# New homes for the merged stream's transposes, for two tail units of the output projection and for the convolved projections' weights

## The chip, the cores and the metric

One Trainium2 chip; the kernel runs on one of its cores. The metric is the device time of one execution in microseconds. The core's engines are named as the profile names them: PE (matmuls; PEld is its weight load), DVE (vector), ACT (scalar activations and copies), POOL, and SP, which issues most DMAs.

## The reference

Two layers of a decoder trunk, 256 tokens, model width 1024, all in float32. Cut to what matters:

```python
def hybrid_layer(x, mem_n, ...):
    h = layer_norm(ALPHA * x + 0.5 * swiglu(x, ffn1_w_gu, ffn1_w_down), ...)
    dn_q, dn_k, dn_v, dn_b, dn_a, dn_z, sw_q, sw_k, sw_v, xa_q, gates = split(h @ w_in)
    o_dn = deltanet_branch(dn_q, dn_k, dn_v, ...)   # q, k, v: silu(causal 4-tap convolution over time)
    o_sw = sliding_window_attention(sw_q, sw_k, sw_v, swa_sinks)
    o_xa = memory_cross_attention(xa_q, mem_n, w_mem_kv)
    merged = sum over the 3 branches of sigmoid(gates) * (branch @ w_branch)
    h = layer_norm(ALPHA * h + merged @ w_out, ...)
    return layer_norm(ALPHA * h + 0.5 * swiglu(h, ffn2_w_gu, ffn2_w_down), ...)
```

The normalised q and k of the DeltaNet branch need sums of squares over each head's 128 channels, for which the kernel transposes them to tokens.

## The kernel before

All weights lie in one long stream in memory, in the order of their use, and are read as units of 128 partitions × 1024 floats (512 KB). `unit()` (line 104) takes the next one: SP loads it into one of four `raw` buffers, and `split` (line 121) writes a high part by a cast on ACT (`whi`) and the rest by a subtract on DVE (`wlo`). A product of two split operands is three matmuls on PE: high·high, high·low, low·high (`mm3`). Without `dst` the two parts go to rings of five buffers each, `whi` and `wlo`; with `dst` they go to named tiles, their homes. The cast of a unit can begin when the load has landed and the last reader of its home is through; the load when a `raw` buffer is free, that is after an earlier unit's subtract.

Where a tile lies in a partition (an address inside the 192 KB of each) is settled by its pool: `hT` (the transposed, split activations, moving or stationary operand of the projections) and `u0` to `u9` lie in a low pool, below 74 KB, then come `whi` and `wlo` (74 to 115 KB), and `w0` to `w3`, `u10` to `u13` lie in a high pool, from 149 KB on.

In `mixers` (line 514) PE's instructions are pinned to program order; the other compute engines get an order from a scheduler that goes by priority, and `unit()` asks for its instructions 300 places ahead. Each engine then runs its own list in order. SP's loads keep program order.

The stages that matter here:

- The conv stage (lines 535 to 590): `conv` for k, q, v, in this order. Each is two halves of two units; a unit is 24 matmuls of 256 columns (stationary the weights, moving `hT`; the profile's names for a matmul's inputs give the moving operand first). Each half goes through `use`: a scale on ACT (L540), three taps on DVE (L543) for each of its two blocks, and a silu on ACT (L544) into the transposed kT, qT or vT (`u0`, `u1`, `u8`). In between stand the transposes to tokens on PE: `tok_k` behind the third unit of q, `tok_q` behind the third unit of v (L133, 8 transposes each), followed by squares on ACT (L564) and reductions on DVE (L565). The next projections of `hT` (xq and sw's q and k) follow.
- The merge (lines 975 to 1037): `branch(2, oT)` multiplies the last branch's output by its weights; for each of four banks DVE applies the gate (L988) and POOL adds it to the merged stream `mg` (L990); `merge_turn` transposes `mg` on PE (L133) into `sm` banks, two of which there are, and splits it into four tiles `mgT`, two for the high and two for the low part.
- The output projection (line 1040): `projA` over 8 units; two lead ones go through `whi`/`wlo`, and six tail units have homes of their own. Stationary operand is `mgT`, moving the weights, 512 columns a matmul. `between(0)` makes the last `merge_turn` and ends the pinning.

Places in the conv stage are told by numbers that the program gives its tiles: conv units 8 to 11 (v) have the raw buffers 2396, 2426, 2467 and 2514, the five units behind them 2600, 2630, 2663, 2705 and 2738; `t_417` and `t_430` are q's halves, `t_438` and `t_450` v's.

Of the kernel before, what the change touches and what calls it, by code (L numbers as in the profile page):

```python
# [2 lines left out]

# [1 line left out]

# [6 lines left out]
F32R = mybir.dt.float32r  # L12
# [5 lines left out]
P = 128  # L18
D = 1024
S = 256  # L20
# [18 lines left out]
def tile_trunk(ctx, tc, x, xT, mem, memT_, wst, lnp, memln, cvw, rows, cst, out):  # L39
# [6 lines left out]
    pu = ctx.enter_context(tc.tile_pool(name="pu", bufs=1))  # L46
# [8 lines left out]
    def nm(s):  # L55
        uid[0] += 1
        return f"{s}_{uid[0]}"
# [4 lines left out]
    def T(pool, shape, tag, dt=F32, bufs=None):  # L62
        pool = pn if pool is pu and tag in NEAR else pool
        kw = {} if bufs is None else {"bufs": bufs}
        return pool.tile(shape, dt, tag=tag, name=nm(tag), **kw)

    def acc():
        return T(psA, [P, 512], "acc")
# [35 lines left out]
    def unit(w=U, dst=None, cuts=1, behind=None):  # L104
        ahead = tc.high_priority(offset=AHEAD) if pos[0] >= 8 * P * U else nullcontext()
        raw = T(praw, [P, U], "raw")
        src = wst[pos[0]:pos[0] + P * w].rearrange("(p w) -> p w", p=P)
        pos[0] += P * w
        (ph, th), (pl, tl) = dst or ((phi, "whi"), (plo, "wlo"))
        with ahead:  # L110
            hi = T(ph, [P, U], th, F32R)
            lo = T(pl, [P, U], tl, F32R)
            for i in range(cuts):
                c = slice(i * w // cuts, (i + 1) * w // cuts)
                nc.sync.dma_start(raw[:, c], src[:, c])
                with tc.issue_after(behind) if behind else nullcontext():
                    newest[:] = split(hi[:, c], lo[:, c], raw[:, c])
        return hi, lo

    def split(hi, lo, src):  # L120
        return nc.scalar.copy(hi, src).ins, nc.vector.tensor_tensor(lo, src, hi.bitcast(F32), op=ALU.subtract).ins  # L121
# [7 lines left out]
    def matmul(*a, **k):  # L129
        return pe(nc.tensor.matmul(*a, **k))  # L130
# [16 lines left out]
    def projB(xt, nt, kpu, behind=None):  # L147
        g = projB_parts(xt, nt, kpu, behind)
        while True:
            try:  # L150
                next(g)
            except StopIteration as e:
                return e.value

    def projB_parts(xt, nt, kpu, behind=None):
        banks = [acc().rearrange("p (t s) -> p t s", t=2) for _ in range((nt + 1) // 2)]
        for uu in range(KD // kpu):
            hi, lo = unit(behind=behind)
            for kk in range(kpu):
                k = uu * kpu + kk  # L160
                for t in range(nt):
                    c = (kk * nt + t) * P
                    o = banks[t // 2][:, t % 2, :]
                    lastt = t % 2 == 1 or t == nt - 1
                    matmul(o, hi[:, c:c + P], xt[0](k), start=(k == 0 and t % 2 == 0), stop=False, skip_group_check=True)
                    matmul(o, hi[:, c:c + P], xt[1](k), start=False, stop=False, skip_group_check=True)
                    matmul(o, lo[:, c:c + P], xt[0](k), start=False, stop=(k == KD - 1 and lastt), skip_group_check=True)
            yield
        return banks

    def halves(xt, use):

        for i in range(2):
            (b,) = yield from projB_parts(xt, 2, 4)
            use(i, b)

    def projA(xt, w, kpu, nk, outs, tail=0, dsts=(), lead=0, after=None, behind=None, held=(), led=None, along=None, ends=()):
# [46 lines left out]
    def full_rows():  # L224

        a, b, c, d = (acc() for _ in range(4))
        return [[a, b], [c, d]], [at()[:, 0:S] for _ in range(2)]
# [13 lines left out]
    def acc_of(t):  # L241
        return (lambda k: t[0][:, k, :], lambda k: t[1][:, k, :])

    def to_T(put, tb, src, q):

        ps = sm()
        for j in range(4):
            k = q * 4 + j
            transpose(ps[:, j * P:(j + 1) * P], src[:, k * P:(k + 1) * P], ident)
        hi, lo = put(q)  # L250
        ts = slice(tb * P, (tb + 1) * P)
        split(hi[:, :, ts], lo[:, :, ts], ps.rearrange("p (j t) -> p j t", j=4))
# [261 lines left out]
    def mixers(l, hT, mkT, mv_, post):  # L514
        xt = acc_of(hT)
# [7 lines left out]
        for tb in range(2):  # L523
            a, b = outs[tb]
# [7 lines left out]

        silu = []

        def conv(seg, dst):
            def use(i, b):
                yc = T(p2, [P, 2, S], "t2", bufs=4)
                for j in range(2):
                    w = cw[:, l, seg * 4 + 2 * i + j, :]
                    nc.scalar.activation(yc[:, j, :], b[:, j, :], AF.Copy, scale=w[:, 3:4])  # L540
                    for t in (2, 1, 0):
                        d = 3 - t
                        nc.vector.scalar_tensor_tensor(yc[:, j, d:], b[:, j, :S - d], w[:, t:t + 1], yc[:, j, d:], op0=ALU.mult, op1=ALU.add)  # L543
                silu[:] = [nc.scalar.activation(dst[:, 2 * i:2 * i + 2, :], yc, AF.Silu).ins]  # L544
            return halves(xt, use)


        kT, qT, vT = (T(pu, [P, 4, S], tag) for tag in ("u0", "u1", "u8"))
# [34 lines left out]
        def tok_q():  # L583
            for tb in range(2):
                sumsq(tok(qT, tb), ssq[:, 1, tb, :])
            nc.vector.tensor_scalar(qeps, ssq[:, 1], RMS_EPS, RMS_EPS * P, ALU.add, ALU.mult)

        weave(conv(1, kT), {})
        weave(conv(0, qT), {3: [tok_k]})
        weave(conv(2, vT), {3: [tok_q]})  # L590


# [218 lines left out]
        def use_sq(i, b):  # L811
            split(*(t[:, 2 * i:2 * i + 2, :] for t in sq_), b)

        weave(halves(xt, use_xq), {3: [tok_v]})
        (b,) = projB(xt, 1, 8)
        for kv in range(2):
            hs = slice(kv * 64, kv * 64 + 64)
            split(swk[0][hs, kv, :], swk[1][hs, kv, :], b[hs, 0, :])
        weave(halves(xt, use_sq), {
            1: [decay],  # L820
            2: [lambda: spread(0), lambda: x_scores(0)],
# [133 lines left out]
        mg, mgT, gts = [], [], {}  # L955
# [68 lines left out]

        def merge_turn(tb, q):
            if not mgT:
                mgT.extend(T(pu, [P, 4, S], f"w{i}", F32R) for i in range(4))
            to_T(lambda q: (mgT[q], mgT[2 + q]), tb, mg[tb], q)

        weave(branch(2, oT), {  # L1030
            3: [lambda: merge_turn(0, 0)],
            4: [lambda: merge_turn(0, 1), lambda: merge_turn(1, 0)]})

        def between(tb):
            if tb == 0:
                merge_turn(1, 1)
                pinned[0] = False

        outs, ends = full_rows()
        projA((lambda k: mgT[k // 4][:, k % 4, :], lambda k: mgT[2 + k // 4][:, k % 4, :]), D, 1, KD, outs, 6,  # L1040
              [((pu, a), (pu, b)) for a, b in (("u6", "u7"), ("u10", "u11"), ("u12", "u13"), ("u0", "u1"), ("u2", "u3"), ("u8", "u9"))], 2, post, led=between, ends=ends)


    hT = new_hT()
# [25 lines left out]
    ends = None  # L1070
    for l in range(NL):
        mT = []
        mid = memory_T(mT, l)
        if l == 0:

            more = {4: lambda *a: xres(0), 6: lambda *a: xres(1), 8: lambda *a: small()}
        post = Post(lnp[l, 0, 0], lnp[l, 0, 1])
        f1.rest(hT, 4, [((pu, "u0"), (pu, "u1")), ((pu, "u2"), (pu, "u3"))], post, mid, ends, {} if l else more)
        kv = memory_kv(mT, post.end)
        if l == 0:  # L1080
            nc.scalar.activation(nea, rw[:, :, 8:12], AF.Exp)
            nc.vector.tensor_scalar(nea, nea, -1.0, None, ALU.mult)
        post2 = Post(lnp[l, 1, 0], lnp[l, 1, 1])
        mixers(l, post.hT, *kv, post2)
        f2 = Ffn()
        begin(f2, post2.hT)
        last = l == NL - 1
        post = Post(lnp[l, 2, 0], lnp[l, 2, 1], last)
        f2.rest(post2.hT, 6, [((pu, a), (pu, b)) for a, b in (("u0", "u1"), ("u2", "u3"), ("u4", "u5"), ("u6", "u13"))], post, behind=post2.end)
        ends = post.end  # L1090
        if not last:
            f1, hT = Ffn(), post.hT
            begin(f1, hT)
# [87 lines left out]
```

## Time and profile before

| | us |
|---|---|
| median of 3 runs | 1281.85 (1281.18 to 1282.19) |
| the profiled execution | 1281.28 |
| its span in the profile | 1279.5 |
| PE busy in it | 1262.5 (99%) |
| DVE busy | 865.1 (68%) |
| ACT busy | 660.3 (52%) |
| POOL busy | 210.9 (16%) |
| mean granted PE clock | 0.997 |

The span begins and ends with the first and last instruction; the execution's own time is 1.8 us longer. All places in time below are us from the span's start. In the rows of a timeline the columns are start, length, engine, line, operation, output<-inputs, shapes, the number of instructions, and in brackets the idle time of the engine just before and what ended it.

### The profile page before, as it was taken

The page shows a single profiled execution, that of the slowest core. Times are in us where ns is not written, and L with a number is a line of the kernel's source. Part 1 is how long each engine was busy: PE and PEld are TensorE (multiplying, and loading weights), DVE is VectorE, ACT ScalarE, POOL GpSimd, SP SyncE. Part 2 cuts the span into 40 slices and gives each one's busy share as a digit, 9 for nine tenths or more (in the row PEclk, how much of TensorE's full clock was granted, in tenths as well). Part 3 has the DMA queues.
Part 4 walks back from the last instruction along what each step waited for, and adds up shares of the span by engine and source line. Part 5 has one row for each costly group of instructions (what it writes and reads, how often), then busy time and mean ns, then how long its engine had stood idle before and what let it go on. Part 6 is the DMA issues. An engine that isn't in the chain of part 4 may idle for free.

```text
span 1279.5 us, 18763 instructions
## 1 busy us (share of the span) xinstructions
PE 1262.5 (99%) x6948; PEld 1074.8 (84%) x6948; DVE 865.1 (68%) x1271; ACT 660.3 (52%) x980; POOL 210.9 (16%) x365
## 2 busy tenths in 40 slices
PE   9999999999999999999999999999999999999997
PEld 6888889999878788888888888899987787888886
DVE  6678576886647776665676665759867388766565
ACT  6556444655665535444454554456656654445441
POOL 0232000002311202221012220010033102122200
PEclk9999999999999999999999999999999999999999
DMA  8888765655434728886657876456464266487762
GB/s 297 304 272 283 254 206 163 210 166 139 160 116 151 260 90 266 243 240 217 227 200 246 256 253 220 176 186 210 152 164 137 95 194 218 168 242 245 236 224 86
DMA packets 77499, 261.40 MB, mean 204 GB/s; under 512 B 11904, under 2 KB 13056, under 8 KB 77408
## 3 DMA queue, kind: packets, MB, share of 16 engines
q1 hardware_dynamic: 66320, 232.53, 55.4%
q0 software_dynamic: 11088, 27.68, 8.1%
q8 instruction: 54, 0.88, 0.3%
q14 instruction: 37, 0.30, 0.1%
HBM read 246.40 MB, written 13.76 MB: 203 GB/s over the span
## 4 chain that ended last, share of the span: by engine, by line
PE 93%; DVE 2%; DMA 2%; ACT 1%; issue 1%; POOL 0%; SPq 0%; DVEq 0%; ACTq 0%; POOLq 0%
PE acc L130 82%; PE at L130 4%; PE sm L130 3%; DMA raw<-in_wst_dram 2%; PE sm L133 1%; DVE wlo L121 1%; PE acc L323 1%; PE acc L324 1%; PE acc L326 1%; ACT whi L121 1%; PE at L133 1%; DVE u L121 0%; POOL u L990 0%; ACT u L121 0%; DVE gt L988 0%
## 5 line engine op out<-in xcount | busy, mean ns | idle before, releaser
L121 DVE TENSOR_TENSOR wlo<-raw,whi 128x1024 fp32r<-128x1024 f32 (+2 forms) x403 | 488.3, 1220 | 281.0 <-ACT whi L121 279.2
L121 ACT CAST whi<-raw 128x1024 fp32r<-128x1024 f32 (+2 forms) x403 | 412.7, 1033 | 399.2 <-PE acc L130 318.8
L130 PE MATMUL acc<-whi,hT 128*128 128x512 f32 (+1 forms) x1824 | 562.6, 386 | 0.6 <-ACT whi L121 0.6
L130 PEld LDWEIGHTS acc<-whi,hT 128*128 128x128 f32 x1824 | 340.2, 188 | 70.0 <-ACT whi L121 2.4
L130 PE MATMUL acc<-wlo,hT 128*128 128x512 f32 (+1 forms) x912 | 350.2, 384 | 0.7 <-DVE wlo L121 0.7
L130 PE MATMUL acc<-whi,u 128*128 128x512 f32 x784 | 248.9, 392 | 0.0
L130 PEld LDWEIGHTS acc<-wlo,hT 128*128 128x128 f32 x912 | 171.3, 188 | 33.9 <-DVE wlo L121 1.7
L130 PEld LDWEIGHTS acc<-whi,u 128*128 128x128 f32 x784 | 147.2, 188 | 30.6
L130 PE MATMUL acc<-wlo,u 128*128 128x512 f32 x392 | 152.7, 390 | 0.0
L353 POOL DMA_DIRECT2D tr<-t x176 | 96.5, 555 | 303.7 <-DVE t L347 293.2
L130 PE MATMUL acc<-hT,whi 128*128 128x256 f32 x672 | 122.2, 284 | 0.0
L130 PEld LDWEIGHTS acc<-hT,whi 128*128 128x128 f32 x672 | 104.6, 192 | 0.0
L130 PE MATMUL acc<-hT,wlo 128*128 128x256 f32 x336 | 95.0, 283 | 0.0
L130 PEld LDWEIGHTS acc<-wlo,u 128*128 128x128 f32 x392 | 73.7, 188 | 14.8
L130 PEld LDWEIGHTS acc<-hT,wlo 128*128 128x128 f32 x336 | 64.3, 191 | 0.0
L354 POOL DMA_DIRECT2D pt<-tr x44 | 25.1, 570 | 199.1 <-DMA tr<-t 133.1
L344 ACT ACTIVATE t<-acc 128x256 f32<-128x256 f32 x88 | 33.5, 381 | 37.7 <-PE acc L130 37.6
L990 POOL TENSOR_TENSOR u<-u,gt 128x512 f32<-128x512 f32 x16 | 24.3, 1527 | 131.1 <-DVE gt L988 131.1
L345 DVE TENSOR_TENSOR t<-t,acc 128x256 f32<-128x256 f32 x88 | 36.6, 416 | 8.8 <-ACT t L344 5.3
L121 DVE TENSOR_TENSOR u<-pt,u 128x512 fp32r<-128x512 f32 x44 | 28.9, 657 | 15.9 <-ACT u L121 15.9
L121 ACT CAST u<-pt 128x512 fp32r<-128x512 f32 x44 | 27.0, 613 | 18.3 <-DMA pt<-tr 18.3
L121 DVE TENSOR_TENSOR u<-raw,u 128x1024 fp32r<-128x1024 f32 x24 | 30.9, 1290 | 7.9 <-ACT u L121 7.8
(236 smaller groups left out, 1210.1 us busy)
## 6 DMA issues: line engine op xcount, KB each, us to landing
raw<-in_wst_dram SPq DMA_DIRECT2D x409, 512.0 KB, 4.4
tr<-t POOLq DMA_DIRECT2D x176, 64.0 KB, 3.9
pt<-tr POOLq DMA_DIRECT2D x44, 256.0 KB, 5.1
raw<-in_wst_dram SPq DMA_DIRECT2D x16, 324.0 KB, 2.9
gB<-in_lnp_dram SPq DMA_DIRECT2D x6, 512.0 KB, 5.6
bB<-in_lnp_dram SPq DMA_DIRECT2D x6, 512.0 KB, 6.0
w<-dr POOLq DMA_DIRECT2D x4, 512.0 KB, 10.7
t<-in_xT_dram SPq DMA_DIRECT2D x4, 256.0 KB, 5.2
```

The costliest lines, as they stand in the source:

```text
L121: return nc.scalar.copy(hi, src).ins, nc.vector.tensor_tensor(lo, src, hi.bitcast(F32), op=ALU.subtract).ins
L130: return pe(nc.tensor.matmul(*a, **k))
L133: return pe(nc.tensor.transpose(*a))
L323: nc.tensor.matmul(ps, hT[0][:, k, ts], hi[:, c], start=k == 0, stop=False)
L324: nc.tensor.matmul(ps, hT[0][:, k, ts], lo[:, c], start=False, stop=False)
L326: nc.tensor.matmul(ps, hT[1][:, k, ts], hi[:, c], start=False, stop=k == KD - 1)
L344: act = nc.scalar.activation(t[:, :, tb, :], g, AF.Silu).ins
L345: ins = nc.vector.tensor_tensor(t[:, :, tb, :], t[:, :, tb, :], u, op=ALU.mult).ins
L353: nc.gpsimd.dma_start(d[:, :, q].rearrange("b c x -> c b x"), z[32 * q:32 * q + 32].rearrange("c (b x) -> c b x", b=4))
L354: back = nc.gpsimd.dma_start(y, d.rearrange("b c q x -> (b c) (q x)")).ins
L990: nc.gpsimd.tensor_tensor(mg[tb][:, js], mg[tb][:, js], gt[tb][:, js], op=ALU.add)
```

## The change

Three things get other homes; no arithmetic is added or removed.

1. The 12 units of the conv stage no longer take the next `whi`/`wlo` buffers, but go round three pairs of homes in the high pool: (`w0`, `w1`), (`w2`, `w3`), (`u12`, `u13`).
2. The transposed, split merged stream `mgT` lies in `u0` to `u3` (low) instead of `w0` to `w3` (high).
3. The last three tail units of the output projection, which had (`u0`, `u1`), (`u2`, `u3`), (`u8`, `u9`), now have (`u8`, `u9`), (`w0`, `w1`), (`w2`, `w3`).

```diff
+from itertools import cycle
...
-    def projB_parts(xt, nt, kpu, behind=None):
+    def projB_parts(xt, nt, kpu, behind=None, homes=None):
...
-            hi, lo = unit(behind=behind)
+            hi, lo = unit(behind=behind, dst=homes and next(homes))
...
-    def halves(xt, use):
+    def halves(xt, use, homes=None):
...
-            (b,) = yield from projB_parts(xt, 2, 4)
+            (b,) = yield from projB_parts(xt, 2, 4, homes=homes)
...
+        homes = cycle(((pu, a), (pu, b)) for a, b in (("w0", "w1"), ("w2", "w3"), ("u12", "u13")))
...
-            return halves(xt, use)
+            return halves(xt, use, homes)
...
-                mgT.extend(T(pu, [P, 4, S], f"w{i}", F32R) for i in range(4))
+                mgT.extend(T(pu, [P, 4, S], f"u{i}", F32R) for i in range(4))
...
-              [((pu, a), (pu, b)) for a, b in (("u6", "u7"), ("u10", "u11"), ("u12", "u13"), ("u0", "u1"), ("u2", "u3"), ("u8", "u9"))], 2, post, led=between, ends=ends)
+              [((pu, a), (pu, b)) for a, b in (("u6", "u7"), ("u10", "u11"), ("u12", "u13"), ("u8", "u9"), ("w0", "w1"), ("w2", "w3"))], 2, post, led=between, ends=ends)
```

With the first hunks the line numbers grow by one to three: the split is L122, the transposes L134, the scale, taps and silu L543, L546 and L547, the gate L991.

What that does to the engines' lists, at three places. First ACT in the conv stage of layer 0, from the squares of tok_k to the silu of q's second half (`u_386<-t_430`). Before:

```order
L564 ACTIVATE t_425_2337<-sm_2332 128x512
L121 CAST whi_2601<-raw_2600 128x1024
L540 ACTIVATE t_430_2385<-acc_2292,cw 128x256
L544 ACTIVATE u_386_2071<-t_417_2282 128x512
L121 CAST whi_2631<-raw_2630 128x1024
L540 ACTIVATE t_430_2385<-acc_2292,cw 128x256
L121 CAST whi_2664<-raw_2663 128x1024
L540 ACTIVATE t_438_2456<-acc_2395,cw 128x256
L544 ACTIVATE u_386_2071<-t_430_2385 128x512
```

And now:

```order
L567 ACTIVATE t_425_2337<-sm_2332 128x512
L122 CAST whi_2601<-raw_2600 128x1024
L122 CAST w_441_2468<-raw_2467 128x1024
L543 ACTIVATE t_430_2385<-acc_2292,cw 128x256
L122 CAST whi_2631<-raw_2630 128x1024
L122 CAST u_448_2515<-raw_2514 128x1024
L547 ACTIVATE u_386_2071<-t_417_2282 128x512
L122 CAST whi_2664<-raw_2663 128x1024
L543 ACTIVATE t_438_2456<-acc_2395,cw 128x256
L122 CAST whi_2706<-raw_2705 128x1024
L122 CAST whi_2739<-raw_2738 128x1024
L543 ACTIVATE t_430_2385<-acc_2292,cw 128x256
```

The casts of conv units 10 and 11 (raw 2467 and 2514), which stood ahead of this piece, now stand in it, each behind the cast of a unit that is used later; the casts of 2706 and 2739 have come ahead of the second scale of `t_430`. Then DVE in the same place, from the subtract behind which q's second half begins to its last tap. Before:

```order
L121 TENSOR_TENSOR wlo_2602<-raw_2600,whi_2601 128x1024
L574 RECIPROCAL rk_391_2076<-ssq_2073 128x8
L256 TENSOR_SCALAR kn_2077<-ssq_2073 128x8
L543 SCALAR_TENSOR_TENSOR t_430_2385<-acc_2292,cw,t_430_2385 128x255
L257 TENSOR_SCALAR kn_2077<-kn_2077 128x8
L543 SCALAR_TENSOR_TENSOR t_430_2385<-acc_2292,cw,t_430_2385 128x254
L259 SCALAR_TENSOR_TENSOR knt_2342<-kn_2077 128x8
L543 SCALAR_TENSOR_TENSOR t_430_2385<-acc_2292,cw,t_430_2385 128x253
L260 TENSOR_TENSOR knt_2342<-knt_2342,ssq_2073 128x8
L121 TENSOR_TENSOR wlo_2632<-raw_2630,whi_2631 128x1024
L261 SCALAR_TENSOR_TENSOR kn_2077<-knt_2342,kn_2077 128x8
L543 SCALAR_TENSOR_TENSOR t_430_2385<-acc_2292,cw,t_430_2385 128x255
```

And now, up to the first tap of the half's second block:

```order
L122 TENSOR_TENSOR u_449_2516<-raw_2514,u_448_2515 128x1024
L576 TENSOR_SCALAR ssq_2073<-ssq_2073 128x8
L546 SCALAR_TENSOR_TENSOR t_430_2385<-acc_2292,cw,t_430_2385 128x255
L577 RECIPROCAL rk_391_2076<-ssq_2073 128x8
L122 TENSOR_TENSOR wlo_2665<-raw_2663,whi_2664 128x1024
L257 TENSOR_SCALAR kn_2077<-ssq_2073 128x8
L546 SCALAR_TENSOR_TENSOR t_430_2385<-acc_2292,cw,t_430_2385 128x254
L122 TENSOR_TENSOR wlo_2707<-raw_2705,whi_2706 128x1024
L258 TENSOR_SCALAR kn_2077<-kn_2077 128x8
L546 SCALAR_TENSOR_TENSOR t_430_2385<-acc_2292,cw,t_430_2385 128x253
L260 SCALAR_TENSOR_TENSOR knt_2342<-kn_2077 128x8
L122 TENSOR_TENSOR wlo_2740<-raw_2738,whi_2739 128x1024
```

The subtracts of 2663, 2705 and 2738 stood behind the last tap of `t_430`; now they stand between its first taps and the taps of its second block, which are interleaved with those of `t_438`. PE's list is the same there as before. The second layer's lists are changed in the same way.

Third, DVE at the merge of layer 0, between the gates of the last branch's third and fourth bank (`acc_4232` and `acc_4258`). Before:

```order
L121 TENSOR_TENSOR u_783_4356<-raw_4354,u_782_4355 128x1024
L988 SCALAR_TENSOR_TENSOR gt_3941<-gt_3941,acc_4232 128x512
L121 TENSOR_TENSOR u_786_4362<-raw_4360,u_785_4361 128x1024
L121 TENSOR_TENSOR w_753_4249<-sm_4251,w_751_4247 128x4x128
L121 TENSOR_TENSOR wlo_4307<-raw_4305,whi_4306 128x1024
L121 TENSOR_TENSOR u_789_4368<-raw_4366,u_788_4367 128x1024
L988 SCALAR_TENSOR_TENSOR gt_3941<-gt_3941,acc_4258 128x512
```

And now:

```order
L991 SCALAR_TENSOR_TENSOR gt_3941<-gt_3941,acc_4232 128x512
L122 TENSOR_TENSOR w_786_4362<-raw_4360,w_785_4361 128x1024
L122 TENSOR_TENSOR u_753_4249<-sm_4251,u_751_4247 128x4x128
L122 TENSOR_TENSOR wlo_4307<-raw_4305,whi_4306 128x1024
L122 TENSOR_TENSOR w_789_4368<-raw_4366,w_788_4367 128x1024
L122 TENSOR_TENSOR u_783_4356<-raw_4354,u_782_4355 128x1024
L991 SCALAR_TENSOR_TENSOR gt_3941<-gt_3941,acc_4258 128x512
```

The third gate stood behind the subtract of the unit with raw 4354 (home `u0`, `u1` before, `u8`, `u9` now); this subtract now stands last, ahead of the fourth gate, and the units in `w0` to `w3` come first. Two smaller moves go with it: on PE the last four transposes of the merged stream (`sm_4317`) come four matmuls later, and on SP the load of the layer norm's offsets (`bB`) comes eight loads earlier, right behind that of its scales (`gB`).

## The prediction

> **What bounds the kernel now.** I read the page first, its busy shares and its chain of waits.
>
> ```profile
> PE 1262.5 (99%) x6948; PEld 1074.8 (84%) x6948; DVE 865.1 (68%) x1271; ACT 660.3 (52%) x980; POOL 210.9 (16%) x365
> ...
> PE 93%; DVE 2%; DMA 2%; ACT 1%; issue 1%; POOL 0%; SPq 0%; DVEq 0%; ACTq 0%; POOLq 0%
> ```
>
> PE is busy 1262.5 of 1279.5 us and carries 93% of the chain that ended last. So the time changes in two ways only: the pitch of matmuls changes, or PE comes to wait. To see where a wait is near, I read the windows of the conv stage in each layer, and of the two places ahead of the output projection (busy time of each engine, then granted clock, DMA share, GB/s).
>
> ```profile
> 226.70:259.30 32.60, 32.60 (x274) 32.60 (x273) 29.89 (x53) 20.22 (x31) 1.35 (x1) 1.00 0.62 201
> 859.70:892.50 32.80, 32.80 (x276) 32.80 (x275) 29.68 (x53) 20.73 (x32) 1.35 (x1) 1.00 0.63 205
> ...
> 432.30:435.80 3.50, 3.50 (x11) 2.91 (x12) 3.50 (x5) 2.57 (x4) 0.72 (x1) 0.51 0.77 239
> ...
> 1065.30:1068.80 3.50, 3.44 (x17) 2.75 (x17) 3.50 (x5) 2.79 (x5) 0.54 (x2) 1.00 0.81 263
> ```
>
> In the conv stage PE never stops, but DVE is busy 29.89 of 32.60 us: 2.7 us of slack in the whole stage. That decides this case. The timelines of PE, ACT and DVE there (start, length, instruction, what ended its idle time):
>
> ```profile
> 246.92 1.03 PE L133 MATMUL sm<-cs,u 128*128 128x128 f32 x8
> ...
> 259.30 1.04 PE L133 MATMUL sm<-cs,u 128*128 128x128 f32 x8
> ```
> ```profile
> 247.00 1.05 ACT L121 CAST whi<-raw 128x1024 fp32r<-128x1024 f32 x1 [0.94 <-PE acc L130]
> ...
> 257.46 0.47 ACT L540 ACTIVATE t<-acc,cw 128x256 f32<-128x256 f32 x1
> 257.83 0.62 ACT L544 ACTIVATE u<-t 128x512 f32<-128x512 f32 x1
> ```
> ```profile
> 248.08 1.23 DVE L121 TENSOR_TENSOR wlo<-raw,whi 128x1024 fp32r<-128x1024 f32 x1 [0.23 <-ACT whi L121]
> 249.22 0.48 DVE L543 SCALAR_TENSOR_TENSOR t<-acc,cw,t 128x255 f32<-128x255 f32 x1
> 249.62 0.68 DVE L565 TENSOR_REDUCE ssq<-t 128x4 f32<-128x512 f32 x1
> 250.21 0.47 DVE L543 SCALAR_TENSOR_TENSOR t<-acc,cw,t 128x254 f32<-128x254 f32 x1
> ...
> 255.85 0.16 DVE L261 SCALAR_TENSOR_TENSOR kn<-knt,kn 128x8 f32<-128x8 f32 x1
> 255.92 0.48 DVE L543 SCALAR_TENSOR_TENSOR t<-acc,cw,t 128x255 f32<-128x255 f32 x1
> ```
>
> The eight transposes at 246.92 are k's (tok_k), those at 259.30 are q's (tok_q). They are pinned in PE's program, tok_q between conv units 10 and 11. tok_q reads the silu at 257.83, which ends at 258.45: only 0.85 us to spare. From start to start DVE takes 1.14 us for a subtract, 0.40 for a tap (L543), 0.59 for a reduction, about 0.08 for a small one.
>
> **The change part by part.** *Conv weights in three homes.* The 12 conv units leave the five whi/wlo buffers, and the five units of the two projections that follow take them. Their splits need no conv matmul to end, so in the program they now stand ahead of the q half that tok_q needs. On ACT the casts of 2664, 2706 and 2739 (the third to fifth of these units) stand ahead of its last scale; on DVE their subtracts stand among its taps. Both engines run in order, so tok_q, and all of PE behind it, waits for them. I first take DVE's work alone, from the subtract at 248.08 (conv unit 9, cast as soon as unit 6 is through, in the new order too) to the last q tap: 8 subtracts × 1.14 = 9.1, 11 taps × 0.40 = 4.4, 2 reductions × 0.59 = 1.2, 12 small ones × 0.08 = 1.0; together 15.7, so 263.8; with the silu's 0.62, 264.4. tok_q stood at 259.30: **a stall of at least 5.1 us in each layer.**
>
> The transfers add to that, because a raw buffer is loaded again only when its subtract is through.
>
> ```profile
> raw<-in_wst_dram SPq DMA_DIRECT2D x9, 512.0 KB, 4.2
> ```
> ```profile
> raw<-in_wst_dram SPq DMA_DIRECT2D x9, 512.0 KB, 3.6
> ```
>
> The first is the median from issue to landing in layer 0 (236 to 262 us), the second in layer 1 (868 to 895). With 4.2: conv unit 8 is cast when unit 5 ends (246.92 − 24 matmuls × 0.12 = 244.04) and subtracted by 246.3; the load of 2600 then lands at 250.5; cast of 2601 250.5, its subtract to 252.8; unit 10 next, to 253.95. Load of 2630 behind unit 9's subtract (249.3): 253.5, subtract to 255.8; unit 11 to 256.95. The load behind 2601's subtract (252.8) lands at 257.0, cast of 2664 to 258.05, subtract to 259.3, a tap to 259.8. The next load, behind unit 10's subtract, is there by 258.15; cast of 2706 to 259.45, subtract 259.75 to 260.95, a tap to 261.45; subtract of 2739's unit to 262.6; five taps and four small ones 2.4: 265.0; silu 265.7. Stall 6.4 us. With 3.6 two loads of that chain come 0.6 earlier each: 5.2, about DVE's own bound; I take 5.3 in layer 1. Both: **+11.7**, between 10.2 (DVE alone) and 14 (landings near 5 us in both layers, as loads now come in pairs).
>
> The splits done early aren't lost, but PE cannot use them to catch up: it was the bound before, and is again after. What is late next is v's half behind tok_q; PE has conv unit 11 and five split units (over 14 us of matmuls) to cover it, so I cost that at nothing; without this cover, some 2.5 us (six taps) a layer.
>
> *The clock.* After an idle 2.56 us (PE row at 432.17, below) the granted clock is 0.51 for 3.5 us; after 2.28 us (1065.36) it stays 1.00. Stalls of over 5 us should bring the dip: 3.5 × 0.49 = 1.7 each, **+3.4**; bounds 0 and 3.4. [...]
>
> *Pitch.* Three triples of rows: conv now (stationary whi, moving hT, both low in the partition), a 256-wide product with one operand high (w), and 512-wide ones with the stationary operand low (u) and high (w).
>
> ```profile
> 229.28 0.40 PE L130 MATMUL acc<-hT,whi 128*128 128x256 f32 x2
> ...
> 236.84 0.40 PE L130 MATMUL acc<-hT,whi 128*128 128x256 f32 x2
> ```
> ```profile
> 189.29 0.40 PE L130 MATMUL acc<-w,whi 128*128 128x256 f32 x2
> ...
> 191.07 0.40 PE L130 MATMUL acc<-w,whi 128*128 128x256 f32 x2
> ```
> ```profile
> 1055.66 0.62 PE L130 MATMUL acc<-whi,u 128*128 128x512 f32 x2
> ...
> 1057.70 0.62 PE L130 MATMUL acc<-whi,u 128*128 128x512 f32 x2
> ```
> ```profile
> 1066.32 0.63 PE L130 MATMUL acc<-whi,w 128*128 128x512 f32 x2
> ...
> 1068.42 0.63 PE L130 MATMUL acc<-whi,w 128*128 128x512 f32 x2
> ```
>
> 7.56 us over 63 matmuls is 120.0 ns, 1.78 over 15 is 118.7; 2.04 over 9 is 226.7, 2.10 over 9 is 233.3. Conv: 576 matmuls × 1.3 ns = −0.75, bounds 0 and twice that. Output projection: 192 matmuls read the merged stream, of which some 84 then have both operands low (× 6.6 ns = −0.55); the rest still read a high operand. Together **−1.4**. [...]
>
> *Ahead of the output projection.* Here PE does wait before, and the new homes put L988 ahead of a late unit.
>
> ```profile
> 429.02 0.60 PE L133 MATMUL sm<-cs,u 128*128 128x128 f32 x4
> 432.17 0.99 PE L133 MATMUL sm<-cs,u 128*128 128x128 f32 x4 [2.56 <-POOL u L990]
> ...
> 437.27 0.60 PE L133 MATMUL sm<-cs,u 128*128 128x128 f32 x4
> ```
> ```profile
> 1065.36 0.66 PE L133 MATMUL sm<-cs,u 128*128 128x128 f32 x4 [2.28 <-POOL u L990]
> 1069.61 0.66 PE L133 MATMUL sm<-cs,u 128*128 128x128 f32 x4 [0.55 <-POOL u L990]
> ```
> ```profile
> 428.03 1.23 DVE L121 TENSOR_TENSOR u<-raw,u 128x1024 fp32r<-128x1024 f32 x1 [2.03 <-ACT u L121]
> 429.17 0.68 DVE L988 SCALAR_TENSOR_TENSOR gt<-gt,acc 128x512 f32<-128x512 f32 x1
> 429.77 1.22 DVE L121 TENSOR_TENSOR u<-raw,u 128x1024 fp32r<-128x1024 f32 x1
> 430.91 0.68 DVE L121 TENSOR_TENSOR w<-sm,w 128x512 fp32r<-128x512 f32 x1
> ```
> ```profile
> 429.93 2.19 POOL L990 TENSOR_TENSOR u<-u,gt 128x512 f32<-128x512 f32 x1 [2.79 <-DVE gt L988]
> ```
>
> PE waits for POOL's L990, that for DVE's L988, and that stood behind the subtract at 428.03. Its bank was full by 426 (12 matmuls, 2.8 us, and four transposes stand between it and the row at 429.02), so it can now run about 2.5 us sooner, and POOL is off the path. The transposes then wait for a free sm bank: the subtract from sm at 430.91 moves little (one subtract stays ahead of it), to 430.45, so they start at about 431.15: 1.0 us sooner, in layer 1 by the like 1.1. Given back: the second L988 stands behind the same subtracts as before and one more than its start allows for, so the last transposes gain only 0.5 to 1.4 us. The load of bB moves eight places up SP's queue; units already split cover it, otherwise about 2 us (512 KB at some 250 GB/s, the last two windows above). Sum: −1.1 and −0.5, **−1.6**; bounds −3.6 (both idle times gone, no dip in layer 0) and +0.5.
>
> Sum: 11.7 + 3.4 − 1.4 − 1.6 = +12.1 on the profiled execution's 1281.28, 1293.4. The median of the runs is 0.57 higher: **1294.0 us.**
>
> **The rivals.** *Stall without dip, at DVE's own bound:* 10.2 − 1.4 − 2 = +6.8, 1288.7. For it: the threshold between 2.28 and 2.56 us is known from two waits only. Against: both stalls are twice that. *A longer stall:* loads in pairs land near 5 us, v's half too is late, or the clock takes two stretches to return: 14 + 3.4 + 4 − 1.5 = +20, 1301.8. DMA is busy 0.62 of the stage, so there is room against it. *Faster:* the q half is in time all the same. The point from which this decides is its last tap by 258.7, which needs the three splits of 2664, 2706 and 2739 (3 × 1.14 us on DVE) and 2 us more to end behind it rather than ahead; then only the gains stay: −3.0, 1278.9. Against it, the order in which both engines have them and their running in order. *The homes do little:* the units pulled ahead find DVE's 2.7 us of slack, and the gains cancel the rest: within 0.2% of before. Against it, the count of 15.7 us of DVE work in a place where 10.6 were free.
>
> **How the numbers follow.** Stall with dips, 1290 to 1298: 0.66. Stall at the bound without dips, 1286 to 1290: 0.14. Longer: 0.12. Homes do little: 0.04. Faster: 0.04. 0.2% (2.6 us) is about what can be told from no change. So faster 0.04, same 0.04, slower 0.92. The range 1287.5 to 1300.5 takes the first two cases nearly whole and the lower part of the longer one.
>
> **What would show it.** In the trace after, tok_q's row at about 259 in layer 0 and 892 in layer 1 starts 5 to 7 us later, released by ACT's silu (L547 there), the chain of waits shows DVE's L122 and the taps there, and the granted clock is near 0.5 for some 3.4 us behind it. The conv window has over 37 us instead of 32.60, with DVE full. The conv pitch is 118.7 ns, that of the first output products 226.7. The transposes once at 432.17 wait 1 to 2 us instead of 2.56. If tok_q starts without a wait, my order of the engines' work is wrong; if it waits under 5 us, my DVE count; if the wait is 8 us or more, the landings.

## The result and the profile after

The changed kernel takes 1296.42 us (median of 4 runs, 1294.84 to 1297.41) against 1281.51 us before (4 runs on the same chip, 1280.34 to 1282.19): a ratio of 1.0119 with a 95% interval of 1.0108 to 1.0131, so 14.9 us slower. The profiled execution is the fastest of the four, 1294.84 us with a span of 1293.0. The page, busy shares and chain of waits:

```profile
PE 1264.8 (98%) x6948; PEld 1076.9 (83%) x6948; DVE 863.8 (67%) x1271; ACT 661.8 (51%) x980; POOL 208.0 (16%) x365
...
PE 90%; DVE 4%; DMA 3%; ACT 2%; issue 1%; POOL 0%; SPq 0%; DVEq 0%; ACTq 0%; POOLq 0%
```

PE's share of the chain went from 93% to 90%; DVE, DMA and ACT have it now. What PE waited for, before in the first block and after in the second (us in total, times, the longest):

```profile
PE sm L133 <- POOL u L990: 5.4, 3, 2.6
```
```profile
PE sm L134 <- ACT u L547: 13.9, 2, 7.5
PE sm L134 <- DVE u L122: 2.2, 2, 1.4
PE sm L134 <- POOL u L993: 0.9, 2, 0.5
```

Two new waits of 13.9 us together, once a layer, for ACT's silu; the waits at the merge went down from 5.4 to 3.1 us. PE's rows at the new waits (layer 0, then layer 1):

```profile
226.72 0.98 PE L131 MATMUL acc<-hT,w 128*128 128x256 f32 x7
...
246.46 1.04 PE L134 MATMUL sm<-cs,u 128*128 128x128 f32 x8
258.57 0.38 PE L134 MATMUL sm<-cs,u 128*128 128x128 f32 x2
265.44 1.54 PE L134 MATMUL sm<-cs,u 128*128 128x128 f32 x6 [6.48 <-ACT u L547]
```
```profile
898.11 0.38 PE L134 MATMUL sm<-cs,u 128*128 128x128 f32 x2
905.95 1.54 PE L134 MATMUL sm<-cs,u 128*128 128x128 f32 x6 [7.46 <-ACT u L547]
```

tok_q comes to its place a little earlier than before (258.57, not 259.30), does the two transposes that need only q's first half, and stops. DVE and ACT ahead of it in layer 0:

```profile
257.25 1.19 DVE L122 TENSOR_TENSOR wlo<-raw,whi 128x1024 fp32r<-128x1024 f32 x1
...
259.04 1.23 DVE L122 TENSOR_TENSOR wlo<-raw,whi 128x1024 fp32r<-128x1024 f32 x1
...
261.10 1.22 DVE L122 TENSOR_TENSOR wlo<-raw,whi 128x1024 fp32r<-128x1024 f32 x1 [0.29 <-ACT whi L122]
...
264.18 0.48 DVE L546 SCALAR_TENSOR_TENSOR t<-acc,cw,t 128x253 f32<-128x253 f32 x1
```
```profile
260.02 1.04 ACT L122 CAST whi<-raw 128x1024 fp32r<-128x1024 f32 x1 [1.01 <-DMA raw<-in_wst_dram]
260.97 0.47 ACT L543 ACTIVATE t<-acc,cw 128x256 f32<-128x256 f32 x1
264.75 0.63 ACT L547 ACTIVATE u<-t 128x512 f32<-128x512 f32 x1 [3.32 <-DVE knt L260]
```

The three subtracts into `wlo` belong to units that PE reads at 271 us or later; q's last tap, behind them, ends at 264.66 and the silu at 265.38. The clock ahead of the first wait, in the waits and behind them (windows; the granted clock stands ahead of the DMA share). It is full ahead of the wait, falls to a mean of 0.86 and 0.74 within the waits, and is 0.50 and 0.59 right behind them:

```profile
226.72:258.57 31.85, 31.85 (x274) 31.85 (x273) 25.21 (x38) 19.56 (x29) 2.48 (x3) 1.00 0.59 187
258.95:265.44 6.49, 0.01 (x2) 0.01 (x1) 6.04 (x20) 2.16 (x5) 0.00 (x0) 0.86 0.77 282
265.44:269.90 4.46, 4.46 (x21) 4.46 (x22) 2.96 (x7) 2.13 (x4) 0.00 (x0) 0.50 0.05 16
...
268.90:272.30 3.40, 3.40 (x24) 3.40 (x24) 0.35 (x1) 0.47 (x1) 0.00 (x0) 0.77 0.00 0
```
```profile
898.10:905.90 7.80, 0.39 (x4) 0.15 (x2) 5.92 (x19) 3.19 (x5) 0.00 (x0) 0.74 0.75 253
905.90:909.40 3.50, 3.45 (x19) 3.45 (x20) 2.98 (x8) 2.19 (x4) 0.00 (x0) 0.59 0.09 33
```

The sum for the profiled pair, by how far PE's instructions of the same number stand apart in the two traces: the conv stage of layer 0 moves PE by +8.3 us, the merge and output projection of layer 0 by −2.3, the conv stage of layer 1 by +8.25, its merge by −0.75; 13.5 us, the difference of the spans (1293.0 − 1279.5).

### The profile page after: what moved, and what is told of

The parts are those of the page before. It is cut to its first block, busy times and chain, and to the rows that moved or that the text cites. A ratio compares the mean times of both kernels' runs of the same rounds, so it can differ in the third digit from the quotient of the medians.

```text
span 1293.0 us, 18745 instructions
## 1 busy us (share of the span) xinstructions
PE 1264.8 (98%) x6948; PEld 1076.9 (83%) x6948; DVE 863.8 (67%) x1271; ACT 661.8 (51%) x980; POOL 208.0 (16%) x365
## 4 chain that ended last, share of the span: by engine, by line
PE 90%; DVE 4%; DMA 3%; ACT 2%; issue 1%; POOL 0%; SPq 0%; DVEq 0%; ACTq 0%; POOLq 0%
PE acc L131 79%; PE at L131 4%; DMA raw<-in_wst_dram 3%; PE sm L131 3%; DVE wlo L122 2%; PE sm L134 1%; ACT whi L122 1%; PE acc L324 1%; PE acc L325 1%; PE acc L327 1%; PE at L134 1%; DVE u L122 1%; DVE w L122 0%; DVE t L546 0%; ACT w L122 0%
## 5 line engine op out<-in xcount | busy, mean ns | idle before, releaser
L122 DVE TENSOR_TENSOR wlo<-raw,whi 128x1024 fp32r<-128x1024 f32 (+2 forms) x379 | 456.0, 1211 | 275.7 <-ACT whi L122 274.0
L122 ACT CAST whi<-raw 128x1024 fp32r<-128x1024 f32 (+2 forms) x379 | 388.3, 1032 | 373.4 <-PE acc L131 287.6
L131 PE MATMUL acc<-whi,u 128*128 128x512 f32 x816 | 259.8, 393 | 0.2
L131 PE MATMUL acc<-hT,whi 128*128 128x256 f32 x288 | 52.7, 285 | 0.0
L131 PE MATMUL acc<-hT,w 128*128 128x256 f32 x384 | 46.8, 280 | 0.0
L131 PEld LDWEIGHTS acc<-hT,w 128*128 128x128 f32 x384 | 45.8, 188 | 0.0
L131 PE MATMUL acc<-u,u 128*128 128x512 f32 x180 | 45.1, 393 | 0.0
L131 PEld LDWEIGHTS acc<-hT,whi 128*128 128x128 f32 x288 | 44.8, 192 | 0.0
L131 PE MATMUL acc<-hT,wlo 128*128 128x256 f32 x144 | 40.8, 283 | 0.0
L546 DVE SCALAR_TENSOR_TENSOR t<-acc,cw,t 128x255 f32<-128x255 f32 (+2 forms) x72 | 35.1, 488 | 8.1 <-ACT t L543 7.0
```

## Experiments

Theory A is that of the prediction: splits that run ahead delay q's second half. Its rivals are told in the expectations. Each kernel was timed beside the kernel before on one chip.

**One part at a time.** The conv weights' homes alone:

```diff
 # the changed kernel, with the merge as before
-                mgT.extend(T(pu, [P, 4, S], f"u{i}", F32R) for i in range(4))
+                mgT.extend(T(pu, [P, 4, S], f"w{i}", F32R) for i in range(4))
...
-              [((pu, a), (pu, b)) for a, b in (("u6", "u7"), ("u10", "u11"), ("u12", "u13"), ("u8", "u9"), ("w0", "w1"), ("w2", "w3"))], 2, post, led=between, ends=ends)
+              [((pu, a), (pu, b)) for a, b in (("u6", "u7"), ("u10", "u11"), ("u12", "u13"), ("u0", "u1"), ("u2", "u3"), ("u8", "u9"))], 2, post, led=between, ends=ends)
```

> The conv weights' homes alone; the merged stream and the tail units as in the kernel before. Theory A (the freed whi/wlo buffers let five later splits run ahead of q's second half; ACT and DVE in order, PE waits at tok_q): tok_q waits 6 to 8 us in each layer as in the changed kernel, each wait followed by about 3.4 us at half clock; the output projection as before. 1281.5 + 13.9 (waits of the changed kernel) + 3.6 (dips) - 1.3 (pitch) = 1297.7, so +16 us. Theory B (the stall needs the moved tail units or the moved merged stream as well, for instance through where they lie): less than +8 us here. The difference to the changed kernel is what its other two parts bring: 1.5 to 3 us.

Measured: 1297.72 against 1281.38, ratio 1.0127 (1.0111 to 1.0142); the waits at tok_q 6.53 and 6.41 us. So these homes alone make the loss, as theory A says, and theory B falls. The other two parts alone are the inverse edit, conv as before:

> The merged stream in u0 to u3 and the tail units' new homes, conv as before. Theory A: no wait in the conv stage; the gate L988 runs ahead of a late subtract at the merge, PE's waits there fall from 5.4 us to about 3 us and there is no half clock in layer 0: -2.3 us in layer 0 and -0.7 us in layer 1 as in the changed kernel, 1278.5. Theory C (this gain comes about only since the conv stage shifted the loads): no change, 1281.5.

Measured: 1279.13, ratio 0.9982 (0.9972 to 0.9991), faster by 2.3 us; no wait in the conv stage. The waits at the merge of layer 0 are those of the changed kernel:

```profile
431.32 0.63 PE L133 MATMUL sm<-cs,u 128*128 128x128 f32 x4 [0.90 <-DVE u L121]
436.67 0.66 PE L133 MATMUL sm<-cs,u 128*128 128x128 f32 x4 [0.47 <-POOL u L990]
```

Theory C falls. The two parts add up: +16.3 − 2.3 = +14.0, against 14.9 in one.

**What in the merge gains.** Only the order of the tail units' homes, the merged stream left high:

```diff
-              [((pu, a), (pu, b)) for a, b in (("u6", "u7"), ("u10", "u11"), ("u12", "u13"), ("u0", "u1"), ("u2", "u3"), ("u8", "u9"))], 2, post, led=between, ends=ends)
+              [((pu, a), (pu, b)) for a, b in (("u6", "u7"), ("u10", "u11"), ("u12", "u13"), ("u8", "u9"), ("u0", "u1"), ("u2", "u3"))], 2, post, led=between, ends=ends)
```

> The kernel before with the last three tail units' homes in another order: (u8,u9), (u0,u1), (u2,u3); the merged stream stays in w0 to w3, conv as before. Theory A: what gains at the merge is the order (the gate ahead of the late subtract), so most of the merge-only kernel's gain is here too: -1.5 to -2.5 us, 1279 to 1280. Theory D: the gain is the matmuls' pitch with the merged stream low in the partition; then nothing here, 1281.4, and PE waits 5.4 us at the merge as before.

Measured: 1279.84 against 1281.71, ratio 0.9985 (0.9974 to 0.9996). The waits at the merge sum to 3.0 us (2.1 for DVE, 0.9 for POOL). The gain is the order; where the merged stream lies adds nothing that the times can show, and theory D falls.

**Holding the splits back.** The changed kernel, with the splits of the four xq units and the one behind them queued behind the silu of q's second half:

```diff
         weave(conv(0, qT), {3: [tok_k]})
+        q_done = silu[0]
...
-        weave(halves(xt, use_xq), {3: [tok_v]})
-        (b,) = projB(xt, 1, 8)
+        weave(halves(xt, use_xq, behind=q_done), {3: [tok_v]})
+        (b,) = projB(xt, 1, 8, q_done)
```

> The changed kernel, but the splits of the xq units and of the unit behind them are issued only after the silu of q's second half; three homes, buffers and addresses stay. Theory A: the wait at tok_q is gone (work ahead of it on DVE falls from 15.7 to about 9 us), at most 3 us a layer come back at tok_v, as four subtracts then stand ahead of v's taps; 1281.5 - 3 (merge) - 1.3 (pitch) = 1277.2, up to 1283 with the waits at tok_v. Theory B' (three homes instead of five buffers are too few, the conv units themselves are split too late): the wait at tok_q stays near 7 us, about 1296.

Measured: 1289.76 against 1281.38, ratio 1.0073 (1.0058 to 1.0088). PE's transposes in layer 0:

```profile
258.42 1.04 PE L134 MATMUL sm<-cs,u 128*128 128x128 f32 x8
270.76 0.38 PE L134 MATMUL sm<-cs,u 128*128 128x128 f32 x2
275.10 1.54 PE L134 MATMUL sm<-cs,u 128*128 128x128 f32 x6 [3.96 <-ACT u L547]
```

tok_q runs through with three homes, so three homes are not too few for the conv units themselves, and theory B' falls. But the wait is at tok_v now, 3.96 and 3.95 us where I had allowed 3: four subtracts stand together ahead of v's taps. The time is 6.8 us above the 1283 that I had allowed; half clock behind each of these waits (two 256-wide matmuls take 0.63 us there, 0.40 ahead of the wait), which I had not counted, is part of it.

**A longer road to q.** tok_q two units later in PE's program, the engines' lists ahead of it nearly the same:

```diff
-        weave(conv(2, vT), {3: [tok_q]})
+        weave(conv(2, vT), {})
...
-        weave(halves(xt, use_xq), {3: [tok_v]})
+        weave(halves(xt, use_xq), {1: [tok_q], 3: [tok_v]})
```

> The changed kernel, but tok_q stands two units later in PE's program (behind the first xq unit), so that PE reaches it 5.7 us later; the engines' lists in front of q's second half are nearly the same. Theory A: q's half is ready at about 265.4 (layer 0) all the same and the wait falls from 6.5 and 7.5 us to 1 to 2.5 us a layer, without half clock: 1281.5 - 4.3 + 2 to 5 = 1279 to 1282. Theory B': conv unit 11 and the xq units are themselves late, so PE waits as long in another place: about 1295.

Measured: 1289.04 against 1281.38, ratio 1.0053 (1.0036 to 1.0070). tok_q waits 0.21 and 0.42 us, less than expected; the time lies 7 us above the upper end of my forecast, for one thing since tok_v now waits:

```profile
274.89 1.30 PE L134 MATMUL sm<-cs,u 128*128 128x128 f32 x6 [1.87 <-ACT u L547]
...
910.35 0.88 PE L134 MATMUL sm<-cs,u 128*128 128x128 f32 x6 [1.87 <-ACT u L547]
```

and smaller waits follow further down; half clock, which I had expected to stay away, came behind the wait of layer 0 (a mean clock of 0.56 from 274.80 to 278.20). The late half is the cause, but moving the point where it is needed only moves the wait.

**Five homes instead of three.**

```diff
-        homes = cycle(((pu, a), (pu, b)) for a, b in (("w0", "w1"), ("w2", "w3"), ("u12", "u13")))
+        homes = cycle(((pu, a), (pu, b)) for a, b in (("w0", "w1"), ("w2", "w3"), ("u12", "u13"), ("u4", "u5"), ("u6", "bB")))
```

> The changed kernel with five pairs of homes for the conv weights instead of three (the two more are tiles that are free at that time). Theory A: five homes do not help by themselves, since the five whi/wlo buffers are free for the later splits all the same, and these stand ahead of q's taps again; but the conv units' own splits are no longer held back by PE, so DVE comes to that place earlier: a wait of 2 to 5 us a layer at tok_q, released by ACT's silu, 1283 to 1291. Theory B' (three homes are too few): no wait, 1277 to 1279.

Measured: 1293.78 against 1281.71, ratio 1.0093 (1.0073 to 1.0112), 3 us above the range I gave; the waits at tok_q 4.28 and 3.83 us, inside it. Most of the excess is a wait I had not counted, for a silu ahead of the conv units (L528). ACT's rows in layer 0 show why it is late:

```profile
PE acc L131 <- ACT u L528: 2.8, 2, 1.5
```
```profile
225.52 1.05 ACT L122 CAST u<-raw 128x1024 fp32r<-128x1024 f32 x1 [1.78 <-DMA raw<-in_wst_dram]
226.59 1.28 ACT L528 ACT_TABLE_LOAD   x1
227.88 0.43 ACT L528 ACTIVATE u<-acc 128x316 f32<-128x316 f32 x1
```

The cast of the fourth conv unit, which has a free home now, stands ahead of this silu and waits for its load; in the changed kernel it stands behind, and the table load begins at 223.23. So the conv units' own splits run ahead here of a chain that PE needs sooner.

With more homes the wait at tok_q shrinks and stays: what matters is what runs ahead.

**Fewer subtracts ahead.** The units behind the conv stage get a lead of 40 places in priority instead of 300 (a parameter through `halves` and `projB`):

```diff
-        ahead = tc.high_priority(offset=AHEAD) if pos[0] >= 8 * P * U else nullcontext()
+        ahead = tc.high_priority(offset=lead) if pos[0] >= 8 * P * U else nullcontext()
```

> The changed kernel, but the splits of the units behind the conv stage get a lead of 40 places in priority instead of 300. In the lists six subtracts instead of eight then stand between conv unit 9's and q's last tap. Theory A, by the count: 2 x 1.14 us less to do on DVE, the wait at tok_q falls from 6.5 and 7.5 us to 4.2 and 5.2, each still with half clock: about 4.6 us less than the changed kernel, 1291.5 (1289.5 to 1293.5). If the landings of the loads set the wait instead, it stays as it was, 1295 to 1297.

Measured: 1288.85 against 1280.41, ratio 1.0062 (1.0049 to 1.0075):

```profile
263.29 1.54 PE L134 MATMUL sm<-cs,u 128*128 128x128 f32 x6 [3.83 <-ACT u L547]
```
```profile
900.58 1.54 PE L134 MATMUL sm<-cs,u 128*128 128x128 f32 x6 [3.98 <-ACT u L547]
```

Two subtracts fewer, and 2.65 and 3.48 us less wait, where the count gave 2.3; the time lies 0.7 us below my range. The wait goes with the number of foreign subtracts. That the rest is their loads, which leave that place with them, is likely but not shown.

**Pacing the splits one by one.** First the five units behind the conv stage, each behind another instruction of ACT:

```diff
-        weave(halves(xt, use_xq), {3: [tok_v]})
-        (b,) = projB(xt, 1, 8)
+        weave(halves(xt, use_xq, marks=[silus[3], scales[9], silus[4], scales[11]]), {3: [tok_v]})
+        (b,) = projB(xt, 1, 8, silus[5])
```

> The changed kernel with the splits of the five later units queued one by one on ACT (behind the silu of q's second half, a scale and the silu of v's first half, the last scale and the silu of v's second half), three homes kept. Theory A: no wait at tok_q nor at tok_v, since no more than one foreign subtract stands ahead of any half: 1281.4 - 3 (merge) - 1 (pitch of conv) = 1277.4, between 1276.5 and 1279. If DVE is simply out of time with three homes: waits of 2 to 4 us a layer stay somewhere in the stage, 1281 to 1285.

Measured: 1288.82 against 1281.71, ratio 1.0059 (1.0042 to 1.0076). No wait at tok_q, none at tok_v, and then:

```profile
284.21 0.99 PE L131 MATMUL sm<-g,cs 128*128 128x8 f32 x4 [3.48 <-DVE g L632]
```

The time lies above both forecasts. The wait went to the decay, 3.48 and 3.42 us, whose chain of small instructions on DVE stood behind four splits of the next projection. So I queued these too (against the paced kernel):

```diff
-        (b,) = projB(xt, 1, 8, silus[5])
-        weave(halves(xt, use_sq), {
+        (b,) = projB(xt, 1, 8, scales[11])
+        weave(halves(xt, use_sq, marks=[expd, (expd, gdone), (expd, gdone), (expd, gdone)]), {
```

> The paced kernel, but the splits of the units after the xq projection are queued too: the one behind xq after v's last scale, the four of the next projection on ACT behind the decay's exponential, and the last three of them on DVE behind its last product (g). Three homes kept. Theory A': DVE and ACT are not short of time, each wait so far came from splits that ran ahead of a chain that PE needs sooner; so no wait at tok_q, tok_v or the decay: 1281.6 - 3 (merge) - 1 (conv pitch) = 1277.6, between 1276.5 and 1279.5. Theory E (with three homes the splits come two units later for good, and some chain behind always pays): a wait of 2 to 4 us a layer further down, 1281 to 1286.

Measured: 1282.32 against 1280.41, ratio 1.0012 (0.9999 to 1.0026): of 14.9 us some 2 are left, with the waits at tok_q, tok_v and the decay gone. The trace is of an execution of 1286.00 us, near the upper end of the twelve (1278.70 to 1286.10), so it shows more loss than the median has. The largest new wait in it is

```profile
PE at L133 <- DVE pp L737: 3.5, 2, 2.0
```

2.0 us in the attention products of layer 0 (at 344.98) and 1.5 in those of layer 1. Theory A' had forecast 1279.5 us at most; the time lies in the range of theory E (1281 to 1286), and the new waits are of its kind, at the low end of its 2 to 4 us a layer. So pacing takes away each wait that it is aimed at, but some chain behind pays again, and I did not reach 1277.6. Whether this must be so with three homes, or a better pacing would get there, stays open.

**Where the operands lie.** The changed kernel with `w0` to `w3`, `u12`, `u13` in the low pool and `u4` to `u7` in the high one:

```diff
-    NEAR = {"hT"} | {f"u{i}" for i in range(10)}
+    NEAR = {"hT", "u0", "u1", "u2", "u3", "u8", "u9", "u12", "u13"} | {f"w{i}" for i in range(4)}
```

> The changed kernel with w0 to w3, u12 and u13 in the low pool and u4 to u7 in the high one; the engines' lists are the same as the changed kernel's. The waits at tok_q stay (6 to 8 us a layer). What it is for: the pitch of the conv matmuls. If the pitch goes by where the stationary operand lies, it is back at 120 ns here (from 117.5 in the changed kernel), 0.7 us a layer; if it goes by the ring of homes (fewer buffers, other names), it stays at 117.5.

One execution, 1299.09 us; the waits at tok_q 6.40 and 7.04 us. Its conv stage starts, and reaches tok_k, at

```profile
227.55 2.67 PE L131 MATMUL acc<-hT,w 128*128 128x256 f32 x21
...
247.70 1.04 PE L134 MATMUL sm<-cs,u 128*128 128x128 f32 x8
```

168 matmuls in 20.15 us, 119.9 ns. The changed kernel takes 19.74 us for them (226.72 to 246.46, above), 117.5 ns, and the kernel before 20.14 us, up to tok_k at 246.92 from

```profile
226.78 0.39 PE L130 MATMUL acc<-hT,whi 128*128 128x256 f32 x2
```

So with the same lists and the same ring of homes the pitch is back where it was: in these three traces it goes with where the conv weights lie, 119.9 ns low and 117.5 high. The mean lengths of the 512-wide products show it too, this kernel against the changed one: those that read `w` (low here, high there) take 389 and 390 ns (by `whi` and by `wlo`) against 395 and 396, those that read `u`, four tiles of which lie high here, 395 and 392 against 393 and 390, and those that read `hT`, which stays where it was, 392 and 390 in both. (The addresses given ahead of the prediction are those of the built program. The 192 KB named there as the size of a partition do not fit it: one of its tiles, `gt`, begins at byte 221,664. Nothing is worked out from that figure.)

## Why the prediction was right, and where its sizes were off

- **The stall.** The place (tok_q in both layers), the releaser (ACT's silu) and the cause (subtracts and casts of 2664, 2706 and 2739 ahead of q's taps) came as worked out, and the holding, counting and single-part kernels show the cause. In layer 0 the sum of steps gave 6.4 us and 6.48 was measured; its last steps, subtract of 2739's unit to 262.6 and silu to 265.7, were 262.32 and 265.38. That the two agree to 0.1 us is partly luck: PE, too, came to the wait 0.35 us ahead of the 259.30 reckoned with. (The trace has ten small instructions in the stretch that was counted on DVE, not twelve: 0.2 us.) In layer 1 it gave 5.3, and 7.46 was measured. The mis-sized term is the landing. I took 3.6 us, the median in the trace before of nine loads issued over 27 us; the new order sends them in bunches. For the three issued from 892 to 896 the trace after has

```profile
raw<-in_wst_dram SPq DMA_DIRECT2D x3, 512.0 KB, 6.0
```

and ACT's cast there waited 2.43 us for one of them:

```profile
898.87 1.04 ACT L122 CAST whi<-raw 128x1024 fp32r<-128x1024 f32 x1 [2.43 <-DMA raw<-in_wst_dram]
```

The prediction named "landings near 5 us in both layers, as loads now come in pairs" as a bound and should have taken it as the value.
- **The clock.** Forecast 1.7 us for each stall. Behind the waits PE lost 2.3 us in layer 0 and 1.3 in layer 1 (from tok_q's resumption to tok_v PE took 14.44 and 13.45 us; before, the same work without the two transposes done ahead of the wait took 12.38 − 0.25). That the sum, 3.6 against 3.4, is right is luck: the picture of one dip of 3.5 us behind each wait is not, see the last section.
- **The pitch.** Conv gained 2.4 ns a matmul (119.9 to 117.5), not 1.3: 576 of them −1.4 us instead of −0.75. The single row group I took for a high operand, with 118.7 ns, covered only 15 matmuls, and in it the high tile was the moving operand, where the change moves the stationary one. The output projection's term (−0.55) cannot be told from zero in the times. The traces of the merge-only and the order-only kernel say more, as there the order is the same and the merged stream lies low in the one and high in the other. In layer 0 the first 13 of these matmuls take 3.06 us with it low (from 431.71) and 3.12 with it high (from 430.44), nine later ones 2.15 and 2.18, and behind these the pitch is 232.5 and 232.7 ns. That is about 0.1 us in a layer against a forecast of 0.27, so by these rows the term was some three times too large.
- **The merge.** Forecast −1.6 and the pitch, measured −2.3 and −0.75: in layer 0 the idle time fell from 2.56 to 0.87 and 0.46 us, so the transposes came 1.7 us sooner and not 1.0, and the dip there is gone (clock 1.00 from 430 to 446), as the low end of the range had it; their wait for an sm bank's subtract came as said, as the releaser of the second row shows. Whether half clock follows a wait of some 2 us differs: behind the 2.28 us in layer 1 of the kernel before the clock stays 1.00, behind 1.87 us in the kernel with tok_q later it is 0.56 (last section). The rows of the changed kernel in layer 0:

```profile
437.20 0.60 PE L134 MATMUL sm<-cs,u 128*128 128x128 f32 x4
438.67 0.63 PE L134 MATMUL sm<-cs,u 128*128 128x128 f32 x4 [0.87 <-DVE u L122]
...
444.00 0.66 PE L134 MATMUL sm<-cs,u 128*128 128x128 f32 x4 [0.46 <-POOL u L993]
```

- **What is late next.** I costed v's half at nothing, since PE has conv unit 11 and five split units as cover. In the changed kernel that held: tok_v waits for nothing. It was the first to go when the splits were held behind q (3.96 us).

All terms together: conv +8.3 and +8.25 against my 6.4 + 5.3 + 3.4 − 0.75 = 14.35 for both, the merge −3.05 against −2.15. The likeliest case came true. The sum for the profiled pair, 12.1, fell short of 13.5, and 1294.0 short of the median by 2.4 us; the landings in layer 1 alone are 2.2.

## What to carry to other kernels

Giving one set of tiles homes of their own also frees the buffers that they had, and an order by readiness and priority fills these at once with work that nobody needs yet, ahead of work on the same in-order engine that the busiest engine waits for. Before such a move, count the work that stands ahead of the next chain on the critical engine's path and compare it with the slack in that stage (here 15.7 us of work where 10.6 were free), and take the transfer time of a bunch, not of single loads (here 6.0 us for three issued within 4 us, 3.6 for nine issued over 27). Where an engine has little slack in a stage (here DVE, busy 29.89 of 32.60 us before), holding work back may only hand the wait on to the next chain, as it did in two kernels here (1289.76 and 1288.82 us) and, in smaller part, in a third (1282.32); the cheap gain in this case was one line that ordered the homes at the merge (1.9 us).

## What the runs showed of the hardware that I had not expected

The half clock is no function of the wait's length alone. In the kernel with tok_q later, both layers have the same wait of 1.87 us (rows above), but windows right behind them show half clock in the one and full in the other:

```profile
274.80:278.20 3.40, 3.31 (x17) 3.31 (x18) 2.97 (x13) 1.63 (x4) 0.00 (x0) 0.56 0.74 241
910.30:913.70 3.40, 3.35 (x29) 3.35 (x30) 3.11 (x14) 1.59 (x3) 0.00 (x0) 1.00 0.68 224
```

So my threshold between 2.28 and 2.56 us was none. What sets the two apart no run here shows.

By the traces' record of the granted clock the half clock lasts 3.41 us at the merge before the change (from 432.34) and 6.83 us, twice that, in each layer of the changed kernel (from 263.62 and from 901.91). Windows just inside these three stretches, the first from the trace before, the others from the trace after:

```profile
432.35:435.75 3.40, 3.40 (x11) 2.81 (x11) 3.40 (x5) 2.52 (x4) 0.67 (x1) 0.50 0.76 236
```
```profile
263.63:270.44 6.81, 5.00 (x24) 5.00 (x25) 4.71 (x16) 2.82 (x5) 0.00 (x0) 0.50 0.25 85
...
901.92:908.73 6.81, 2.78 (x13) 2.78 (x14) 6.51 (x21) 2.66 (x6) 0.00 (x0) 0.50 0.50 156
```

In the changed kernel part of it fell inside the wait already: 1.8 us of 6.49 in layer 0 (mean clock 0.86) and 4.0 of 7.80 in layer 1 (0.74); 5.0 and 2.8 us, PE's busy time in the last two windows, are left behind it. That is how the longer wait of layer 1 cost less behind it than the shorter one of layer 0.
